# Block sums of the squared-ReLU activations made by GpSimd in the first MLP product and kept in DRAM, instead of made by VectorE in the second

## The chip, the cores and the metric

The kernel runs on one core of one Trainium2 chip. The metric is the device time of one execution in microseconds (us). Before the change it is 2887.82 us, the median of three runs (2886.27 to 2888.08).

The engines are PE (TensorE, matmul; PEld is its weight load), DVE (VectorE), ACT (ScalarE), POOL (GpSimd) and SP (SyncE, which here only issues DMAs). A DMA can be issued from SP, ACT or POOL; the profile calls those issued from POOL software DMAs.

## The reference

One inference step of a decoder trunk with two layers. Layer 0 is forgetting attention beside an RG-LRU, layer 1 is sparse attention with a lightning indexer. Each layer ends in the part that the change touches:

```python
def sq_relu_ffn(x, w1, w2):
    return jnp.square(jax.nn.relu(x @ w1)) @ w2

hp = hp + sq_relu_ffn(rms_norm(hp, norm_ffn[layer]), ffn_w1[layer], ffn_w2[layer])
hs = hs + sq_relu_ffn(rms_norm(hs, norm_ffn[layer]), ffn_w1[layer], ffn_w2[layer])
```

`hp` has 1024 prompt rows and `hs` 8 sample rows; the kernel puts them side by side, T = 1032 columns. D_MODEL is 1024, D_FF 4096, and all is fp32.

## The kernel before

The work runs with features on the partitions and the T = 1032 columns along the free dimension. Every fp32 product is made of three matmuls on fp32r halves: a value is split into hi (a rounded copy, made by ACT) and lo (value minus hi, a subtraction with two operands in SBUF, made by DVE or POOL), and the product is hi·hi + hi·lo + lo·hi (lines 1489 to 1491).

Both products of the MLP save one multiplication in eight with a Strassen-Winograd scheme: seven block products, numbered i = 0 to 6, in place of eight (`product`, line 1480). It needs sums and differences of blocks of the weights (`Left`, line 1357) and of the right operand. A column half is 2·HP = 516 columns: x1 the first 516, x2 the last.

**First product, "up"** (`up`, line 1522). Sixteen groups g, each of 256 output features, seven products each, 24 matmuls per product. Per group two raw weight tiles `fraw` of 512 KB are loaded by SP (line 1394), multiplied by the norm's gain on POOL (`up_scale`, line 1502, 128x1024), and made into operands `fl` and `fs` five products ahead (`up_make`). The results are evacuated from PSUM into two tiles of 128 features, `za` and `zb` (128x1032, lines 1547 to 1562, ACT and DVE), go through ReLU and the norm's scale on DVE, are squared on ACT (lines 1566 and 1570), and are stored to DRAM by SP as `d_z` (lines 1567 and 1571).

**Second product, "down"** (`down`, line 1659). Seven blocks b of 512 features (groups 2b and 2b+1), in each four outputs op, in each seven products of 12 matmuls: 28 products or 336 matmuls in a block. The last 512 features (groups 14 and 15) are multiplied plainly behind it. At the start of block b SP loads the four tiles `zr` of block b+1 (`z_load`, line 1575). During block b, after every fourth product, `z_make` (line 1580) makes one of the seven right operands of block b+1: it forms the block difference in place in `zr` on DVE where one is needed (i = 1, 2 and 3; eight 128x516 subtractions for each block, lines 1604, 1605, 1607 and 1611), copies hi on ACT (line 1608) and subtracts lo on POOL (line 1609; for block 0 by turns on DVE and POOL). The operands are `zop` (i = 0 to 2) and `zoph` (i = 3 to 6). The weights of block b+1 are prepared six products ahead (`down_make`, line 1615): their sums `s` and `fraw` on POOL (pattern "pppp"), hi on ACT, lo (`fd`, `fdu`, 128x256) on DVE. DVE also adds each product out of PSUM into the residual `xT` or `x1a`/`x1b` (line 1686, two 128x258 additions for each product).

**What sets the order.** The code emits one stream; a scheduler orders each engine's instructions by its own simulated times and gives out the buffers. An engine runs its instructions in that order and waits at the first that is not ready. Most tiles come out of one pool of 22 buffers (`U`, tag "u"): `fraw`, `fs`, `z`, `zr`, `zop`, `fdu` all share it, so that a load can wait for another tile's last reader. The helpers `act`, `tt`, `gt`, `stt` stand in lines 215 to 229 and are the lines by which the profile names ACT, DVE (L218, L229) and POOL (L221) work; `eng` (line 1353) picks POOL for "p" and DVE otherwise.

Of the kernel before, what the change touches and what calls it, by code (L numbers as in the profile page):

```python
# [75 lines left out]
def _r(ap):  # L76
    return ap.bitcast(F32)
# [13 lines left out]
UPLA, DNLA = 5, 6  # L91
ZSUB, ZADD = ("dp" * 7, "p" * 14), ("d" * 7, "d" * 7)
UPE, DNE = ("dddd", "ddddddd"), ("pppp", "ddddddd")
# [66 lines left out]
def build(tc, I, O, C):  # L160
    nc = tc.nc
    with ExitStack() as ctx:
# [1301 lines left out]

        d_z = [dr.tile([32, 128, T], F32, name="d_z%d" % l) for l in range(2)]

        class Ffn:
# [12 lines left out]
            def product(self, ps, left, right, start):  # L1480

                wh, wl = left
                nk = len(right)
                for p in range(2):
                    for k in range(nk):
                        hi, lo = lohi(right[k])
                        cols = slice(p * HP, p * HP + HP)
                        o = ps[p][:, :HP]
                        mm(o, lhsT=wh[:, k], rhs=hi[:, cols], start=(start and k == 0), stop=False, skip_group_check=not start)  # L1489
                        mm(o, lhsT=wh[:, k], rhs=lo[:, cols], start=False, stop=False, skip_group_check=not start)  # L1490
                        i = mm(o, lhsT=wl[:, k], rhs=hi[:, cols], start=False, stop=(k == nk - 1),  # L1491
                               skip_group_check=not start)
                dense[0] = i.ins.name
                return 6 * nk * HP / 2.4


# [25 lines left out]
            def up(self, before):  # L1522
# [3 lines left out]
                for g in range(16):  # L1526
# [3 lines left out]
                    for z, i in enumerate((0, 3, 1, 2, 4, 5, 6) if g == 0 else range(7)):  # L1530
# [33 lines left out]
                        if i == 5:  # L1564
                            stt(za, za, 0.0, rb, MAX, MUL)
                            act(za, za, AF.Square)
                            dma(out=d_z[self.l][2 * g], in_=za)
                        if g == 15:
                            before(z)
                    act(zb, zb, AF.Square)  # L1570
                    dma(out=d_z[self.l][2 * g + 1], in_=zb)
                    self.lefts.pop(g)


            def z_load(self, b):
                q = self.zq[b] = [U([128, T], F32, "zr") for _ in range(4)]
                for j in range(4):
                    dma(out=q[j], in_=d_z[self.l][4 * b + j])

            def z_make(self, b, i):  # L1580
                if i == 0:
                    self.zs[b] = {}
                s = self.zs[b]

                def alloc(i):
                    if i < 3:
                        s[i] = [U([128, T], F32R, "zop") for _ in range(2)]
                    else:
                        if i in (3, 4):
                            h, x = H(F32R, "zoph"), (3, 4)  # L1590
                        else:
                            h, x = H(F32R, "zoph"), (5, 6)
                        for y in range(2):
                            s[x[y]] = [h[:, 2 * y + j] for j in range(2)]

                x1, x2 = slice(0, 2 * HP), slice(2 * HP, 4 * HP)
                for k in {0: (0,), 1: (1,), 2: (2,), 3: (3,), 5: (5,)}.get(i, ()):
                    alloc(k)
                for j in range(2):
                    za, zb = self.zq[b][2 * j], self.zq[b][2 * j + 1]  # L1600
                    src = (za[:, x1], za[:, x1], za[:, x1], zb[:, x1], za[:, x2], zb[:, x2], zb[:, x1])[i]
                    hi, lo = lohi(s[i][j])
                    if i == 1:
                        eng(ZADD[b > 0], i)(za[:, x1], za[:, x2], za[:, x1], SUB)
                        eng(ZADD[b > 0], i)(za[:, x2], zb[:, x2], za[:, x2], SUB)
                    elif i == 2:
                        eng(ZADD[b > 0], i)(za[:, x1], zb[:, x2], za[:, x1], SUB)
                    act(hi, src)
                    eng(ZSUB[b > 0], 2 * i + j)(lo, src, _r(hi), SUB)
                    if i == 3:  # L1610
                        eng(ZADD[b > 0], i)(zb[:, x1], zb[:, x1], za[:, x1], SUB)
                if i == 6:
                    self.zq.pop(b)

# [27 lines left out]
            def before(self, z):  # L1642

                if z == 0:
                    self.zq, self.zs, self.dn_made, self.du = {}, {}, 0, {}
                    self.z_load(0)
                    self.r2.load(1)
# [11 lines left out]
            def down(self):  # L1659
                for i in range(4, 7):  # L1660
                    self.z_make(0, i)
                for b in range(7):
                    if b < 6:
                        self.z_load(b + 1)
                    for op in range(4):
# [4 lines left out]
                        for i in range(7):  # L1670
                            self.down_make(7 * m + i + DNLA)
                            if b < 6 and (7 * op + i) % 4 == 3:
                                self.z_make(b + 1, (7 * op + i) // 4)
                            if i == 1:
# [15 lines left out]
                    if b == 5:  # L1690
# [4 lines left out]
                        for k in range(4):  # L1695
                            dma(out=_r(zl[k]), in_=d_z[self.l][28 + k])
                    if b == 6:
# [916 lines left out]
```

## Time and profile before

| | |
|---|---|
| time, median of 3 runs | 2887.82 us (2886.27 to 2888.08) |
| profiled execution: time, span | 2877.05 us, 2875.2 us |
| busy share of the span | PE 90%, PEld 84%, DVE 76%, ACT 47%, POOL 41% |
| mean granted clock of TensorE | 0.948 of full speed |
| chain that ended last | PE 48%, DVE 23% of the span; its largest DVE entry is `DVE zr L218` with 4% |
| layer 0: up, down | up from about 636 to 958 us, down to about 1298 us |
| layer 1: up, down | up from about 2140 to 2471 us, down to about 2816 us |
| DMA | 318.91 MB, 111 GB/s over the span |

Times below are microseconds from the span's start. A row of a view by windows has the busy time of each engine with its number of instructions in brackets, then the granted clock of TensorE (1.00 is 2.4 GHz, 0.50 is 1.2 GHz), the busy share of the DMA engines, and GB/s. A row of a view by groups has the line, engine, operation, output and inputs, shapes and count, then busy us and mean ns of one, then the idle time of the engine in front of them and what ended it. A row of a timeline has start, duration, engine, line, operation, and in brackets the idle time before it.

### The profile page before, as it was taken

The numbers are of one execution on the slowest core, as the hardware profiler recorded it, in microseconds if no ns is written. First come the engines' busy times: TensorE is split into PE (matmuls) and PEld (weight loads), VectorE is DVE, ScalarE is ACT, GpSimd is POOL, SyncE is SP. The second block draws the span as 40 slices with busy tenths as digits, with TensorE's granted clock in tenths as the row PEclk, the third lists the DMA queues.
The fourth block names the chain that finished last, engine by engine and source line by source line (L and its number), as shares of the span: only waits on it lengthen the run. The fifth ranks groups of instructions, "written<-read, shape, count | busy, mean of one in ns | idle before, by whom it ended". The sixth has DMA issues, their size and how long they took to land.

```text
span 2875.2 us, 48325 instructions
## 1 busy us (share of the span) xinstructions
PE 2576.8 (90%) x17916; PEld 2406.7 (84%) x17916; DVE 2195.1 (76%) x4243; ACT 1341.9 (47%) x2824; POOL 1191.2 (41%) x916
## 2 busy tenths in 40 slices
PE   7988888989999888899888758999969999889998
PEld 6977878979999888899877744567969999788898
DVE  4467897787566999996468899998386565999995
ACT  4236656344343433333255567779244444433331
POOL 2375554242222676730544525033041121667740
PEclk9999899989999999999989868999989999999999
DMA  4854567203232422222353335210313232432221
GB/s 130 265 157 130 162 210 266 95 30 109 98 118 89 147 90 97 89 96 92 89 159 109 113 85 131 75 56 23 111 38 110 97 118 89 133 103 82 96 89 60
DMA packets 254400, 318.91 MB, mean 111 GB/s; under 512 B 23617, under 2 KB 198889, under 8 KB 253909
## 3 DMA queue, kind: packets, MB, share of 16 engines
q1 hardware_dynamic: 207492, 275.68, 29.7%
q10 hardware_dynamic: 39616, 19.93, 2.4%
q0 software_dynamic: 7056, 20.22, 2.4%
q8 instruction: 141, 2.31, 0.3%
q14 instruction: 95, 0.77, 0.1%
HBM read 230.00 MB, written 85.81 MB: 110 GB/s over the span
## 4 chain that ended last, share of the span: by engine, by line
PE 48%; DVE 23%; issue 4%; ACT 3%; DMA 1%; POOL 1%; SPq 0%; DVEq 0%; ACTq 0%; POOLq 0%
PE d L1489 10%; PE d L1491 10%; PE d L1490 10%; DVE zr L218 4%; PE d L341 3%; PE d L339 3%; PE d L340 3%; DVE xT L218 2%; DVE fdu L218 2%; PE s L530 2%; DVE fd L218 2%; PE o L2081 2%; PE t L251 1%; DVE x1a L218 1%; DVE tjk L1975 1%
## 5 line engine op out<-in xcount | busy, mean ns | idle before, releaser
L221 POOL TENSOR_TENSOR fraw<-fraw,small 128x1024 f32<-128x1024 f32 x64 | 142.0, 2227 | 424.4 <-DMA fraw<-in_ffn_w 193.9
L1489 PE MATMUL d<-xoph,fs 128*128 128x258 f32 x768 | 219.0, 285 | 5.9 <-ACT z L215 4.9
L218 DVE TENSOR_TENSOR xT<-xT,d 128x258 f32<-128x258 f32 (+1 forms) x472 | 186.7, 423 | 45.8 <-PE d L341 31.4
L1490 PE MATMUL d<-xoph,fs 128*128 128x258 f32 x768 | 218.8, 285 | 2.6 <-DVE xoph L218 2.6
L1491 PE MATMUL d<-xoph,fs 128*128 128x258 f32 x768 | 218.6, 285 | 2.4 <-DVE fs L218 2.4
L339 PE MATMUL d<-xh,whif 128*128 128x344 f32 (+1 forms) x616 | 202.8, 330 | 5.7 <-DVE small L226 2.4
L341 PE MATMUL d<-xh,wlof 128*128 128x344 f32 (+1 forms) x616 | 198.9, 327 | 6.6 <-DVE wlof L218 6.6
L340 PE MATMUL d<-xl,whif 128*128 128x344 f32 (+1 forms) x616 | 200.9, 326 | 0.0
L215 ACT ACTIVATE s<-s,small 128x128 f32<-128x128 f32 (+7 forms) x192 | 149.5, 781 | 69.5 <-DVE small L533 68.8
L339 PE MATMUL d<-xh,whi 128*128 128x344 f32 x504 | 170.9, 340 | 11.0 <-ACT whi L215 5.5
L341 PE MATMUL d<-xh,wlo 128*128 128x344 f32 x504 | 165.7, 332 | 11.8 <-DVE wlo L218 11.6
L340 PE MATMUL d<-xl,whi 128*128 128x344 f32 x504 | 167.8, 333 | 0.0
L221 POOL TENSOR_TENSOR zoph<-zr,zoph 128x516 fp32r<-128x516 f32 x104 | 156.9, 1522 | 25.5 <-ACT zoph L215 24.6
L1489 PE MATMUL d<-xop,fl 128*128 128x258 f32 x512 | 147.9, 289 | 14.6 <-ACT fl L215 14.6
L1489 PEld LDWEIGHTS d<-xoph,fs 128*128 128x128 f32 x768 | 146.2, 190 | 7.0 <-ACT z L215 5.7
L1491 PEld LDWEIGHTS d<-xoph,fs 128*128 128x128 f32 x768 | 146.7, 191 | 2.9 <-DVE fs L218 2.8
L251 PE MATMUL t<-small,s 128*128 128x128 f32 x864 | 139.8, 280 | 10.4 <-DVE tm L218 3.0
L1490 PEld LDWEIGHTS d<-xoph,fs 128*128 128x128 f32 x768 | 146.4, 191 | 3.2 <-DVE xoph L218 3.2
L1491 PE MATMUL d<-xop,fl 128*128 128x258 f32 x512 | 146.7, 288 | 2.5 <-DVE fl L218 2.5
L1490 PE MATMUL d<-xop,fl 128*128 128x258 f32 x512 | 147.1, 287 | 0.0
L1489 PE MATMUL d<-zoph,fdu 128*128 128x258 f32 x448 | 133.1, 298 | 13.6 <-DVE xT L218 8.4
L221 POOL TENSOR_TENSOR zop<-zr,zop 128x516 fp32r<-128x516 f32 x78 | 117.2, 1512 | 63.4 <-ACT zop L215 36.9
(482 smaller groups left out, 9850.2 us busy)
## 6 DMA issues: line engine op xcount, KB each, us to landing
fraw<-in_ffn_w SPq DMA_DIRECT2D x120, 512.0 KB
d_z<-z SPq DMA_DIRECT2D x64, 516.0 KB
zr<-d_z SPq DMA_DIRECT2D x56, 516.0 KB
kp<-in_cache_fox_kv SPq DMA_DIRECT2D x64, 256.0 KB
vp<-in_cache_fox_kv SPq DMA_DIRECT2D x64, 256.0 KB
q1b<-d_q ACTq DMA_DIRECT2D x32, 512.0 KB
wraw<-in_ab_w_in SPq DMA_DIRECT2D x21, 512.0 KB
wrawf<-in_c_w_in SPq DMA_DIRECT2D x17, 512.0 KB
```

The costliest lines, as they stand in the source:

```text
L215: return nc.scalar.activation(out=out, in_=in_, func=func, **kw)
L218: return nc.vector.tensor_tensor(out=out, in0=a, in1=b, op=op)
L221: return nc.gpsimd.tensor_tensor(out=out, in0=a, in1=b, op=op)
L251: return nc.tensor.transpose(out, in_, ident[:n, :n])
L339: mm(ps, lhsT=wh, rhs=ah, start=(j == 0), stop=False)
L340: mm(ps, lhsT=wh, rhs=al, start=False, stop=False)
L341: i = mm(ps, lhsT=wl, rhs=ah, start=False, stop=(j == last))
L530: mm(p[:, :m], lhsT=lh[x], rhs=ks[:, k0:k0 + m], start=(x == 0), stop=(x == 1 and not dg))
L1489: mm(o, lhsT=wh[:, k], rhs=hi[:, cols], start=(start and k == 0), stop=False, skip_group_check=not start)
L1490: mm(o, lhsT=wh[:, k], rhs=lo[:, cols], start=False, stop=False, skip_group_check=not start)
L1491: i = mm(o, lhsT=wl[:, k], rhs=hi[:, cols], start=False, stop=(k == nk - 1), skip_group_check=not start)
L2081: mm(po[:64], lhsT=VF[g // 2][:, kb, 64 * (g % 2):64 * (g % 2) + 64], rhs=ph, start=(kb == 0), stop=(kb == i))
```

## The change

The plain blocks and the sums are now made once, in the first product, and stored side by side as `d_zp`: for each block b seven slots of 128 x 2 x 516, one for each right operand (the 2 are the groups 2b and 2b+1). In group g < 14, SP stores the first half of `za` (slot 0) and both halves of `zb` (slots 1 and 2); then POOL makes four subtractions 128x516 in place in `za` and `zb` (`z_sums`), and POOL itself issues two DMAs that store the four results (slots 3 to 6). Groups 14 and 15 are stored plainly as before.

In the second product `z_load` fetches one slot (128x1032, 516 KB) for one operand, a few operands ahead (ZLA = 3), and `z_make` has only the hi copy on ACT and the lo subtraction left, each one instruction of 128x1032 in place of two of 128x516. The subtraction is POOL's for b > 0; for block 0 DVE and POOL take turns. The eight DVE subtractions on `zr` per block are gone. A block is read from DRAM as seven tiles of 516 KB instead of four.

```diff
-ZSUB, ZADD = ("dp" * 7, "p" * 14), ("d" * 7, "d" * 7)
+ZSUB, ZLA = ("dpdpdpd", "p" * 7), 3
...
-        d_z = [dr.tile([32, 128, T], F32, name="d_z%d" % l) for l in range(2)]
+        d_z = [dr.tile([4, 128, T], F32, name="d_z%d" % l) for l in range(2)]
+        d_zp = [dr.tile([7, 7, 128, 2, 2 * HP], F32, name="d_zp%d" % l) for l in range(2)]
+        ZSLOT = (0, 3, 6, 1, 4, 2, 5)
...
-                        hi, lo = lohi(right[k])
+                        hi, lo = right[k] if type(right[k]) is tuple else lohi(right[k])
...
+            def zp(self, g, s, n):
+                v = d_zp[self.l][g // 2, s:s + n, :, g % 2]
+                return v[0] if n == 1 else v.rearrange("i p c -> p i c")
+            def z_sums(self, g, za, zb):
+                if g >= 14:
+                    dma(out=d_z[self.l][2 * g - 27], in_=zb)
+                    return
+                x1, x2 = slice(0, 2 * HP), slice(2 * HP, 4 * HP)
+                two = lambda z: z.rearrange("p (i c) -> p i c", i=2)
+                dma(out=self.zp(g, 1, 2), in_=two(zb))
+                gt(za[:, x1], za[:, x2], za[:, x1], SUB)
+                gt(za[:, x2], zb[:, x2], za[:, x2], SUB)
+                nc.gpsimd.dma_start(out=self.zp(g, 3, 2), in_=two(za))
+                gt(zb[:, x2], zb[:, x2], za[:, x1], SUB)
+                gt(zb[:, x1], zb[:, x1], zb[:, x2], SUB)
+                nc.gpsimd.dma_start(out=self.zp(g, 5, 2), in_=two(zb))
...
-                            dma(out=d_z[self.l][2 * g], in_=za)
+                            if g < 14:
+                                dma(out=self.zp(g, 0, 1), in_=za[:, :2 * HP])
+                            else:
+                                dma(out=d_z[self.l][2 * g - 28], in_=za)
...
-                    dma(out=d_z[self.l][2 * g + 1], in_=zb)
+                    self.z_sums(g, za, zb)
...
-            def z_load(self, b):
-                q = self.zq[b] = [U([128, T], F32, "zr") for _ in range(4)]
-                for j in range(4):
-                    dma(out=q[j], in_=d_z[self.l][4 * b + j])
+            def z_load(self, n):
+                while self.zn < min(n, 49):
+                    b, i = divmod(self.zn, 7)
+                    t = self.zq[b, i] = U([128, 2, 2 * HP], F32, "zr")
+                    dma(out=t, in_=d_zp[self.l][b, ZSLOT[i]])
+                    self.zn += 1
             def z_make(self, b, i):
...
+                s = self.zs.setdefault(b, {})
+                if i < 3:
+                    hi, lo = (U([128, 2, 2 * HP], F32R, "zop") for _ in range(2))
+                else:
+                    if i in (3, 5):
+                        self.zh2 = H(F32R, "zoph").rearrange("p k (j c) -> p k j c", j=2)
+                    y = (i - 3) % 2
+                    hi, lo = self.zh2[:, 2 * y], self.zh2[:, 2 * y + 1]
+                s[i] = [(hi[:, j], lo[:, j]) for j in range(2)]
+                self.z_load(7 * b + i + 1)
+                src = self.zq.pop((b, i))
+                act(hi, src)
+                eng(ZSUB[b > 0], i)(lo, src, _r(hi), SUB)
...
-                    self.zq, self.zs, self.dn_made, self.du = {}, {}, 0, {}
-                    self.z_load(0)
+                    self.zq, self.zs, self.dn_made, self.du, self.zn = {}, {}, 0, {}, 0
+                    self.z_load(4)
...
+                self.z_load(7 + ZLA)
                 for b in range(7):
-                    if b < 6:
-                        self.z_load(b + 1)
...
-                                self.z_make(b + 1, (7 * op + i) // 4)
+                                n = (7 * op + i) // 4
+                                self.z_make(b + 1, n)
+                                self.z_load(7 * (b + 1) + n + 1 + ZLA)
...
```

What stands where before and now, at two places. The names carry buffer numbers; the semaphores in brackets are those an instruction waits for (DMAHW: DMAs issued from SP or ACT; DMASW: DMAs issued from POOL; DVE, Activation, PE, Pool: these engines).

First place: POOL in the middle of the first product of layer 0, before (two groups' scalings of raw weights and half of two more):

```order
L221 TENSOR_TENSOR fraw_7845<-fraw_7845,small_75 128x1024 [waits DMAHW0_49,DMAHW2_49,DVE_49,PE_49]
L221 TENSOR_TENSOR fraw_7847<-fraw_7847,small_75 128x1024 [waits DMAHW1_49,DVE_49,Pool_49]
L221 TENSOR_TENSOR fraw_8076<-fraw_8076,small_75 128x1024 [waits DMAHW4_49,DMAHW6_49,DVE_49,PE_49]
L221 TENSOR_TENSOR fraw_8078<-fraw_8078,small_75 128x1024 [waits DMAHW5_49,DVE_49,Pool_49]
L221 TENSOR_TENSOR fraw_8307<-fraw_8307,small_75 128x1024 [waits DMAHW0_49,DMAHW2_49,DVE_49,PE_49]
```

and now, one group's scalings, the sums of the group two earlier and their two stores:

```order
L221 TENSOR_TENSOR fraw_7883<-fraw_7883,small_75 128x1024 [waits DMAHW0_49,DMASW5_49]
L221 TENSOR_TENSOR fraw_7885<-fraw_7885,small_75 128x1024 [waits DMAHW1_49,DMASW6_49]
L221 TENSOR_TENSOR z_7650<-z_7650 128x516 [waits DMAHW2_49,Activation_49]
L221 TENSOR_TENSOR z_7650<-z_7651,z_7650 128x516 [waits Activation_49,Pool_49]
L221 TENSOR_TENSOR z_7651<-z_7651,z_7650 128x516 [waits DMAHW3_49,Pool_49]
L1513 DMA d_zp0_122<-z_7650 128x2x516
L221 TENSOR_TENSOR z_7651<-z_7651 128x516 [waits DVE_49,Pool_49]
L1516 DMA d_zp0_122<-z_7651 128x2x516 [waits Pool_49]
```

Between two pairs of scalings POOL now has four subtractions and two DMA issues. On SP at the same place, before:

```order
L1394 DMA fraw_7845<-in_ffn_w1 128x4x256 [waits DMAHW2_49,DMAHW0_49,PE_49]
L1394 DMA fraw_7847<-in_ffn_w1 128x4x256 [waits DMAHW1_49,DVE_49,Pool_49]
L1567 DMA d_z0_120<-z_7618 128x1032 [waits Activation_49]
L1571 DMA d_z0_120<-z_7619 128x1032 [waits Activation_49]
L1394 DMA fraw_8076<-in_ffn_w1 128x4x256 [waits DMAHW6_49,DMAHW4_49,PE_49]
```

and now:

```order
L1394 DMA fraw_7883<-in_ffn_w1 128x4x256 [waits DMAHW0_49,DMASW5_49,Pool_49]
L1394 DMA fraw_7885<-in_ffn_w1 128x4x256 [waits DMAHW1_49,DMAHW7_49,DMASW6_49,Pool_49]
L1590 DMA d_zp0_122<-z_7650 128x516 [waits DMAHW2_49,Activation_49]
L1510 DMA d_zp0_122<-z_7651 128x2x516 [waits DMAHW3_49,Activation_49]
L1394 DMA fraw_8120<-in_ffn_w1 128x4x256 [waits DMAHW4_49,DMASW7_49,Pool_49]
```

The loads of the next raw weights, which waited for PE, DVE and POOL, now wait for DMASW, that is for POOL's stores of `z` to have landed: they take the buffers of that `za` and `zb`. They stand in front of the next group's stores on SP.

Second place: the second product of layer 0 while the operands of the block b = 3 are made. On DVE before:

```order
L218 TENSOR_TENSOR xT0_4698<-xT0_4698,d_11359 128x258 [waits PE_49]
L218 TENSOR_TENSOR zr_11349<-zr_11349 128x516 [waits DMAHW6_49,Pool_49]
L218 TENSOR_TENSOR xT0_4698<-xT0_4698,d_11360 128x258 [waits PE_49]
L218 TENSOR_TENSOR fd_11523<-fraw_11210,fd_11523 128x256 [waits Activation_49]
L218 TENSOR_TENSOR zr_11351<-zr_11351 128x516 [waits DMAHW0_49,Pool_49]
L218 TENSOR_TENSOR xT1_4699<-xT1_4699,d_11212 128x258 [waits PE_49]
L218 TENSOR_TENSOR zr_11349<-zr_11350,zr_11349 128x516 [waits DMAHW7_49,DVE_49]
L218 TENSOR_TENSOR xT1_4699<-xT1_4699,d_11213 128x258 [waits PE_49]
```

and now, at the same weights of the operand before (the tile named fraw_11210 is fraw_11254 now):

```order
L218 TENSOR_TENSOR fdu_11453<-fraw_11254,fdu_11453 128x256 [waits Activation_49]
L218 TENSOR_TENSOR xT0_4700<-xT0_4700,d_11395 128x258 [waits PE_49]
L218 TENSOR_TENSOR fd_11494<-fraw_11254,fd_11494 128x256 [waits Activation_49]
L218 TENSOR_TENSOR xT0_4700<-xT0_4700,d_11396 128x258 [waits PE_49]
L218 TENSOR_TENSOR fd_11555<-fraw_11254,fd_11555 128x256 [waits Activation_49]
L218 TENSOR_TENSOR xT1_4701<-xT1_4701,d_11256 128x258 [waits PE_49]
L218 TENSOR_TENSOR xT1_4701<-xT1_4701,d_11257 128x258 [waits PE_49]
```

The subtractions on `zr` are gone from between the additions to `xT` and the lo parts `fd` and `fdu`. On POOL at the same place, before:

```order
L221 TENSOR_TENSOR fraw_11210<-s1_11413,fraw_11210 128x2x128 [waits DVE_49,Pool_49]
L221 TENSOR_TENSOR zop_11420<-zr_11349,zop_11420 128x516 [waits DMAHW6_49,Activation_49]
L221 TENSOR_TENSOR zop_11421<-zr_11351,zop_11421 128x516 [waits DMAHW0_49,Activation_49]
L221 TENSOR_TENSOR zoph_11664<-zr_11350,zoph_11664 128x516 [waits DMAHW7_49,Activation_49]
L221 TENSOR_TENSOR zoph_11664<-zr_11352,zoph_11664 128x516 [waits DMAHW1_49,Activation_49]
L221 TENSOR_TENSOR fraw_11210<-fraw_11210 128x2x128 [waits DVE_49,Pool_49]
L221 TENSOR_TENSOR zop_11499<-zr_11349,zop_11499 128x516 [waits PE_49,Activation_49]
L221 TENSOR_TENSOR zoph_11824<-zr_11350,zoph_11824 128x516 [waits PE_49,Activation_49]
L221 TENSOR_TENSOR zoph_11824<-zr_11352,zoph_11824 128x516 [waits Activation_49]
```

and now:

```order
L221 TENSOR_TENSOR fraw_11254<-s1_11449,fraw_11254 128x2x128 [waits DVE_49,Pool_49]
L221 TENSOR_TENSOR zop_11457<-zr_11221,zop_11456 128x1032 [waits DMAHW6_49,Activation_49]
L221 TENSOR_TENSOR zop_11536<-zr_11299,zop_11535 128x1032 [waits DMAHW0_49,Activation_49]
L221 TENSOR_TENSOR fraw_11254<-fraw_11254 128x2x128 [waits DVE_49,Pool_49]
L221 TENSOR_TENSOR zoph_11694<-zr_11460,zoph_11694 128x1032 [waits DMAHW3_49,PE_49,Activation_49]
L221 TENSOR_TENSOR zoph_11694<-zr_11539,zoph_11694 128x1032 [waits DMAHW5_49,Activation_49]
L221 TENSOR_TENSOR s1_11591<-fraw_11393 128x256 [waits DMAHW2_49,PE_49]
```

Fourteen subtractions 128x516 have become seven of 128x1032, in nearly the same stretch between the weights' sums (`s1` and `fraw`).

## Rows read from the trace of the kernel before

**Rows 1.** Busy time of each engine in four windows of layer 0.
```profile
700.00:740.00 40.00, 40.00 (x335) 40.00 (x335) 25.70 (x43) 17.11 (x32) 9.07 (x4) 1.00 0.32 114
958.80:1006.00 47.20, 38.65 (x270) 35.77 (x269) 47.20 (x83) 21.51 (x48) 39.48 (x33) 0.93 0.36 119
1195.50:1243.00 47.50, 43.74 (x338) 43.14 (x338) 45.36 (x94) 18.09 (x42) 34.59 (x31) 0.93 0.21 68
1243.00:1283.00 40.00, 40.00 (x337) 40.00 (x336) 35.30 (x85) 15.40 (x31) 9.79 (x13) 1.00 0.27 94
```

**Rows 2.** The same view, windows of 4 us in a block of layer 1.
```profile
2680.00:2684.00 4.00, 0.60 (x6) 0.43 (x4) 4.00 (x5) 1.16 (x2) 4.00 (x4) 0.90 0.00 0
2684.00:2688.00 4.00, 4.00 (x19) 4.00 (x20) 4.00 (x8) 1.05 (x3) 4.00 (x4) 0.50 0.00 0
...
2712.00:2716.00 4.00, 4.00 (x36) 4.00 (x35) 3.02 (x9) 1.25 (x3) 0.74 (x1) 1.00 1.00 340
```

**Rows 3.** Chain of waits in 950 to 1270: shares, and two pieces.
```profile
by line: DVE zr L218 19.1%; DVE xT L218 16.7%; PE d L1489 12.3%; PE d L1490 11.8%; PE d L1491 11.8%; DVE fdu L218 8.9%; issue 8.6%; DVE fd L218 7.6%; DVE z L229 1.0%; ACT fdu L215 0.7%; DVE zoph L218 0.5%; DVE z L218 0.5%; ACT fd L215 0.3%;
...
1116.68 1.79 DVE zr L218
...
1164.09 1.79 DVE zr L218
```

**Rows 4.** Groups by shape on DVE, 960 to 1240 (second product, layer 0).
```profile
L218 DVE TENSOR_TENSOR xT<-xT,d 128x258 f32<-128x258 f32 x313 | 118.6, 413 | 7.4 <-PE d L1491 7.3
L218 DVE TENSOR_TENSOR zr<-zr 128x516 f32<-128x516 f32 x50 | 64.1, 1282 | 0.0
L218 DVE TENSOR_TENSOR fdu<-fraw,fdu 128x256 fp32r<-128x256 f32 x71 | 47.9, 678 | 0.0
L218 DVE TENSOR_TENSOR fd<-fraw,fd 128x256 fp32r<-128x256 f32 x70 | 46.6, 668 | 0.1
```

**Rows 5.** Groups by shape on POOL in the same window.
```profile
L221 POOL TENSOR_TENSOR zoph<-zr,zoph 128x516 fp32r<-128x516 f32 x49 | 74.3, 1531 | 12.2 <-ACT zoph L215 11.9
...
L221 POOL TENSOR_TENSOR fraw<-fraw 128x256 f32<-128x256 f32 x47 | 40.6, 866 | 17.4 <-DVE fd L218 16.1
```

**Rows 6.** Timeline of DVE late in a block of layer 1.
```profile
2707.13 0.41 DVE L218 TENSOR_TENSOR fdu<-fraw,fdu 128x256 fp32r<-128x256 f32 x1
2707.47 0.41 DVE L218 TENSOR_TENSOR fd<-fraw,fd 128x256 fp32r<-128x256 f32 x1
```

**Rows 7.** Timelines of POOL and of DVE in the first product, layer 1.
```profile
2269.69 1.90 POOL L221 TENSOR_TENSOR fraw<-fraw,small 128x1024 f32<-128x1024 f32 x1 [1.84 <-DMA fraw<-in_ffn_w]
...
2269.80 2.33 DVE L218 TENSOR_TENSOR fl<-fraw,fl 128x512 fp32r<-128x512 f32 x1 [1.29 <-ACT fl L215]
```

**Rows 8.** Instructions of the tiles zr and r1l: lo parts on POOL, ns min/median/max.
```profile
L221 POOL TENSOR_TENSOR zoph<-zr,zoph x104: 1277/1478/2287, 949.1 to 2746.2; 128x516 fp32r<-128x516 f32 x104
...
L221 POOL TENSOR_TENSOR r1l<-raw,r1h x12: 2387/2429/2449, 1397.4 to 1627.6; 128x1032 fp32r<-128x1032 f32 x12
```

**Rows 9.** Timelines of SP, POOL, ACT and DVE in the first product, layer 0.
```profile
750.09 0.94 SPq L1394 DMA_DIRECT2D fraw<-in_ffn_w  x2
757.36 0.34 SPq L1567 DMA_DIRECT2D d_z<-z  x1
...
770.25 0.94 SPq L1394 DMA_DIRECT2D fraw<-in_ffn_w  x2
...
754.34 5.27 POOL L221 TENSOR_TENSOR fraw<-fraw,small 128x1024 f32<-128x1024 f32 x2 [24.65 <-DMA fraw<-in_ffn_w]
...
760.14 0.64 ACT L215 ACTIVATE fs<-fraw 128x512 fp32r<-128x512 f32 x1 [0.26 <-DMA d_z<-z]
...
767.34 0.69 DVE L218 TENSOR_TENSOR s<-fraw 128x512 f32<-128x512 f32 x1 [0.97 <-PE d L1490]
```

**Rows 10.** Line 865: POOL's own DMAs of 512 KB in the attention of layer 0.
```profile
L865 POOL DMA_DIRECT2D qst<-d_q x16: 713/735/781, 90.2 to 480.6; - x16
...
DMA to landing us min/median/max: 4.3/7.7/11.1
```

More of the change, by code (lines that the diff above doesn't have):

```diff
@@ L1570, in up @@
                     act(zb, zb, AF.Square)
-                    dma(out=d_z[self.l][2 * g + 1], in_=zb)
+                    self.z_sums(g, za, zb)
                     self.lefts.pop(g)
-            def z_load(self, b):
-                q = self.zq[b] = [U([128, T], F32, "zr") for _ in range(4)]
-                for j in range(4):
-                    dma(out=q[j], in_=d_z[self.l][4 * b + j])
-            def z_make(self, b, i):
[L1581 to L1613, printed above, removed]
@@ L1695, in down @@
                         for k in range(4):
-                            dma(out=_r(zl[k]), in_=d_z[self.l][28 + k])
+                            dma(out=_r(zl[k]), in_=d_z[self.l][k])
                     if b == 6:
```

## The prediction

> **What bounds the kernel now.** I read the windows by stage first, then the chain of waits, then the groups and timelines of the engines that end a wait. In the first product PE is busy without a gap: 335 matmuls in 40 us, 0.1194 us each, with DVE at 25.7 and POOL at 9.1 of 40 us [rows 1]. Nothing there is won by making DVE lighter, and whatever is added there must stay hidden. In the second product a block is 336 matmuls, 40.1 us at that rate. The last block, which prepares no successor, reaches it (337 in 40 us). The blocks before it take 47.4 us: the window 1195.5 to 1243 holds 338 matmuls in 47.5 us with DVE busy for 45.4 and POOL for 34.6 [rows 1], and in the chain the same `zr` subtraction comes back 47.4 us later (1116.68, 1164.09) [rows 3]. Preparing the next block thus costs 7.3 us.
>
> How it costs that is seen in windows of 4 us: PE gets 6 matmuls while DVE and POOL are both busy throughout; then, PE having stood, the granted clock is 0.50 (the level of 1.2 GHz) for 4 us with 19 matmuls [rows 2]. The chain names DVE: `zr` has 19.1% of 320 us, 61 us, more than any other line [rows 3]. So DVE is what ends last, and `zr` is what the change takes from it.
>
> **Second product, what goes.** Per block DVE does 56 additions out of PSUM, 28 lo parts `fd`/`fdu` and 8 `zr` subtractions. The `zr` group has 1.282 us each, 10.3 us per block. The additions keep 0.413 us, but `fd` and `fdu` take 0.68 on average [rows 4], while two of them undisturbed take 0.41 and start 0.34 apart [rows 6]. So POOL holds each of the 28 up by some 0.26, 7.3 us per block.
>
> **Second product, what changes.** POOL's fourteen lo parts of 128x516 (1.53 us) become seven of 128x1032; its 16 weight sums per block (0.87) stay [rows 5]. The long form is in the trace elsewhere, 2.43 us where DVE is quiet; the short form has 1.28 at its fastest [rows 8], so beside a busy DVE I add the same 0.23 to the long one: 2.66. POOL goes from 14 x 1.53 + 16 x 0.87 = 35.3 us per block to 7 x 2.66 + 13.9 = 32.5. POOL is not the bound.
>
> The point that speaks against the change is what a longer POOL instruction does to DVE. In one place DVE's `fl`, 0.69 us alone [rows 9], took 2.33 because a POOL instruction of 1.90 us had started 0.11 before it [rows 7]: it waited 1.64 us, nearly all of it. The Trainium skill, SBUF — State Buffer, section "SBUF: two separate sides", says that a DVE instruction with two SBUF inputs and a GpSimd one lock each other out for a whole instruction and do not share the port; this place agrees. If the port were shared instead, the wait would go with POOL's busy time and fall to 6.7 us per block, and PE alone would bound the block.
>
> With whole instructions waited for, the wait per `fd` grows with the number of POOL instructions times their length squared, over the block's time. Before: 14 x 1.53² = 32.8 and 16 x 0.87² = 12.1, so 73% of the 7.3 us come from `z` parts. After: 7 x 2.66² = 49.5, and the block is nearer 41.5 than 47.4 us. The `z` share grows by 1.72, the rest by 1.14: 7.3 x (0.73 x 1.72 + 0.27 x 1.14) = 11.4 us. DVE's block is then (56 + 28) x 0.335 + 11.4 = 39.5 us. Before, DVE was busy 45.4 of 47.5 us, so 2.1 us went idle while the block was bound by it; I keep them: 41.6. Bounds: if no `fd` waits longer than now, DVE has 28.1 + 7.3 + 2.1 = 37.5 and PE's 40.1 stands; if each of the seven long ones holds DVE for the 86% seen at `fl`, the wait is 7 x 2.29 + 2.2 = 18.2, and the block is 48.4, 1 us worse than now. I take 41.6, 5.8 us less per block, nearer to the PE end because DVE's own `zr` work is gone for certain.
>
> Five blocks in each of two layers (b = 1 to 5): 10 x 5.8 = 58 us. I take layer 1 as layer 0; rows 2, of layer 1, show the same stall. Block 0 is worse now: 270 matmuls (32.2 us) in 47.2 us with DVE busy for all of it [rows 1], 15 us lost; 5.8 of them go likewise, 12 us for two layers. The sums of block 0 in front of it go from DVE too; I count nothing there (0 to 8 us).
>
> Reading 7 x 516 + 4 x 512 KB per block is 137 GB/s, where a window shows 340 [rows 2]; loads run three operands ahead, each operand being due every four products (5.7 us). SP issues three loads more per block and ACT has fewer instructions: nothing for either. Hidden under the matmuls; if that cover went, the operand that is late would show as an ACT wait for `zr`.
>
> **First product, what is added.** Per group POOL gets four subtractions of about 1.3 to 1.5 us and two DMA issues of 0.74 [rows 8, 10], 7.1 us in 20.1, on top of 4.5 [rows 1]. DVE's two-input work can wait behind them, but the operands are made five products (14 us) ahead and DVE has 14 of 40 us free, so nothing is charged for that. Behind the subtractions on POOL stands the next scaling of `fraw`, and the load of that `fraw` on SP waits until POOL's stores have landed.
>
> The timing of that loop: a pair of loads was issued at 750.09, POOL scaled from 754.34 to 759.61, and the first use of the result was at 767.34 [rows 9]. So there are 7.7 us of slack. The sums come right behind the scaling: three subtractions, an issue, a fourth, an issue, so `zb` is issued at 759.6 + 4 x 1.4 + 0.74 = 766.0 and its buffer is free at 766.0 + X, X being landing. The load that takes it went out at 770.7. A full round is X + 6.4 (sums) + 4.3 (load to scaling) + 2.6 (one scaling): X + 13.3, against a period of 20.1; so X up to 6.8 is free. X is not in this stage's trace. Nearest rows: POOL's own DMAs of the same size have 4.3, 7.7 and 11.1 (least, median, most) [rows 10]; SP's store of 516 KB at 757.36 had landed by 760.14, 2.8 us [rows 9]. At 7.7 a round is 0.9 us too long: twelve rounds, 10.8 us less the slack of 7.7, 3 us per layer. I take that, 6 us in all; bounds 0 (X at 4.3) and, at 11.1, 12 x 4.3 - 7.7 = 44 per layer, 88.
>
> **The sum.** -58 - 12 + 6 = -64 us against the profiled execution's 2877.05 (span 2875.2, 1.9 us around it). That execution is 10.8 us under the median of the runs shown, 2887.82; the difference is carried over: 2824 us.
>
> **The rivals.**
> *PE alone bounds the second product.* DVE's relief is 10.3 us per block and 7.3 would do. Every block falls to 40.1: 10 x 7.3 + 2 x 12 (block 0 keeps 3 of its 15) and no loss in the first product, 97 us: 2791. For it: DVE does nothing on POOL's account in over half of a block [rows 6]. Against it: the work for the next block comes bunched, which is where PE stood [rows 2].
> *The long POOL instructions eat it.* A wait of 16 us gives DVE 28.1 + 16 + 2.1 = 46.2: 1.2 us per block, 12 us, 4 more in block 0, 6 lost: 2878. For it: `fl` [rows 7].
> *The stores through POOL set the pace of the first product.* Slower: PE, without a gap now, begins to wait for `fraw`, scaled too late because its buffer is still being stored. It decides from X = 9.8: 2 x (12 x (X - 6.8) - 7.7) then equals the 70 us won in the second product. At 11.1 it is 88 - 70 = 18 us slower, 2906. For it: half of POOL's DMAs took over 7.7 us [rows 10]. Against: when these stores go out, no weight load is in flight (they are issued 750 and 770, the stores about 763 and 766). The Trainium skill, same page and section, calls this a trap: descriptors of GpSimd's DMAs are written through that shared port, so that a store of 0.62 us stood 3.1 us beside a DVE copy. No row shows this by itself; by that 2.5 us more on 4.3, X would be 6.8, just at the edge.
>
> **How the numbers follow.** The forecast, 2805 to 2845, has 0.46. PE alone: 0.2. Long instructions: 0.18, spread over 2850 to 2895 with a third of it beyond no change. The loop: 0.14. 0.02 is for what I have not seen. 0.2% (6 us) is about what can be told from no change. Faster: 0.46 + 0.2 + 0.12 = 0.78; within 0.2%: 0.06; slower: 0.16. The range 2788 to 2893 leaves out the loop's cases and little below.
>
> **What would show it.** The second product's blocks should be 41 to 42 us long, `zr` absent from DVE, `fd` and `fdu` at 0.75 to 0.85 us mean, the clock at 1.00 in nearly every window. The additions out of PSUM should still be what PE waits for, if it waits. In the first product PE should stay at 335 in 40 us; POOL there should be at 23 of 40, and `fraw` should wait for its DMA with no PE gap behind. I am wrong if PE has gaps in the first product that end in POOL's scaling (the loop), if blocks stay at 45 us or more with `fd` above 0.9 (long instructions), or if an operand waits for its load of `zr`.

## The result, and the profile after

The median is 2848.53 us (4 runs, 2839.99 to 2850.07) against 2887.95: a ratio of 0.9866, interval 0.9854 to 0.9878, 39 us less where 64 were forecast. It lies 3.5 us outside the likeliest band of the prediction (2805 to 2845) and just short of the one of the rival with the long POOL instructions (2850 to 2895). By stage, from the starts of the matmuls in the two traces (the first product from its first matmul, 624.9 and 2124.9 us before and 628.9 and 2121.4 after; then end of one product to end of the next):

| us | before | after | change | forecast |
|---|---|---|---|---|
| first product, layers 0 and 1 | 333.8, 346.2 | 334.6, 345.9 | +0.5 | +6 |
| second product, layer 0 | 339.5 | 326.7 | -12.8 | -35 |
| second product, layer 1 | 344.6 | 318.2 | -26.4 | -35 |

That is -38.7, near the 39.4 between the medians. The two profiled executions differ by 27.7 only: ahead of, between and behind the two MLPs the later one took 11 us more. The profiled execution of the kernel before, 2877.05, stands among runs on a chip where the median was 2877.49; beside the changed kernel it was 2887.95. Between the MLPs, 826.7 became 831.3 us; further kernels with the order of the changed one there took 824 to 836. So the 11 us may be the chip or spread; no run tells them apart.

The view by windows, columns as in [rows 1]: a stretch of the first product, block 0 of layer 0, a steady block, the last block.

```profile
700.00:740.00 40.00, 40.00 (x335) 40.00 (x335) 29.40 (x43) 16.28 (x30) 23.84 (x17) 1.00 0.49 164
963.40:1020.80 57.40, 45.59 (x340) 43.55 (x338) 54.63 (x91) 24.85 (x47) 37.10 (x28) 0.94 0.54 184
1111.10:1155.90 44.80, 41.49 (x338) 40.63 (x338) 42.31 (x85) 17.44 (x36) 30.07 (x24) 1.00 0.34 116
1246.20:1286.20 40.00, 40.00 (x333) 40.00 (x332) 35.47 (x80) 14.22 (x24) 6.80 (x9) 1.00 0.24 71
```

In this window the first product is as full as before, with POOL at 23.8 of 40. A steady block is 44.8 us, between the 47.4 of [rows 3] and the 41.6 forecast. Its parts, windows of 4 us:

```profile
1114.00:1118.00 4.00, 2.93 (x24) 2.75 (x24) 4.00 (x8) 1.19 (x3) 2.90 (x3) 1.00 0.32 117
1118.00:1122.00 4.00, 3.21 (x27) 3.01 (x26) 4.00 (x7) 0.49 (x1) 4.00 (x2) 1.00 0.01 2
...
1130.00:1134.00 4.00, 2.57 (x21) 2.26 (x20) 4.00 (x7) 1.12 (x2) 4.00 (x3) 1.00 0.00 0
...
1142.00:1146.00 4.00, 4.00 (x35) 4.00 (x34) 3.49 (x10) 1.56 (x4) 2.27 (x3) 1.00 0.03 9
...
1150.00:1154.00 4.00, 4.00 (x35) 4.00 (x35) 2.73 (x8) 0.71 (x3) 1.32 (x2) 1.00 0.46 130
```

The loss lies where POOL makes its `z` parts: in three such windows PE gets 21 to 27 of 35 matmuls, and DVE is busy throughout. Later in the block PE is full and DVE has time left. PE's gaps are shorter than in [rows 2], and the clock stays at 1.00. What PE's matmuls waited for in five steady blocks of layer 1 (us in total, times, longest) was DVE's additions, and neither POOL nor a load:

```profile
PE d L1491 <- DVE x1a L218: 16.3, 17, 1.5
```

The chain over 950 to 1270, as [rows 3]: `zr` is gone, `fdu` has its place, and one piece comes back every 44.8 us.

```profile
by line: PE d L1491 19.4%; PE d L1493 18.5%; PE d L1492 18.5%; DVE fdu L218 15.1%; DVE xT L218 10.4%; issue 8.7%; DVE fd L218 5.1%; POOL zoph L221 1.6%; DVE zoph L218 0.9%; DVE z L229 0.6%; POOL zop L221 0.5%; DVE z L218 0.3%; POOL s L221 0
...
1066.31 3.22 DVE fdu L218 x2
1111.08 3.21 DVE fdu L218 x2
...
1155.86 3.20 DVE fdu L218 x2
```

Groups by shape on DVE, then on POOL, 960 to 1240, as [rows 4, 5]:

```profile
L218 DVE TENSOR_TENSOR xT<-xT,d 128x258 f32<-128x258 f32 x325 | 122.9, 414 | 13.0 <-PE d L1493 12.1
L218 DVE TENSOR_TENSOR fdu<-fraw,fdu 128x256 fp32r<-128x256 f32 x75 | 76.8, 1036 | 0.0
L218 DVE TENSOR_TENSOR fd<-fraw,fd 128x256 fp32r<-128x256 f32 x74 | 53.1, 720 | 0.2
```

```profile
L221 POOL TENSOR_TENSOR zoph<-zr,zoph 128x1032 fp32r<-128x1032 f32 x25 | 64.0, 2570 | 1.0 <-ACT zoph L215 1.0
```

`fdu` went from 0.68 to 1.04 us. One of them on DVE beside POOL's `zoph`, both ending within 0.3 us (a line of DVE's timeline and one of POOL's):

```profile
1129.49 2.65 DVE L218 TENSOR_TENSOR fdu<-fraw,fdu 128x256 fp32r<-128x256 f32 x1
...
1129.24 2.62 POOL L221 TENSOR_TENSOR zoph<-zr,zoph 128x1032 fp32r<-128x1032 f32 x1
```

The first product on SP and POOL:

```profile
753.59 3.57 SPq L1394 DMA_DIRECT2D fraw<-in_ffn_w  x2
...
752.70 0.73 POOL L1516 DMA_DIRECT2D d_zp<-z  x1 [0.30 <-POOL z L221]
758.35 1.92 POOL L221 TENSOR_TENSOR fraw<-fraw,small 128x1024 f32<-128x1024 f32 x1 [4.93 <-DMA fraw<-in_ffn_w]
```

The second of SP's two loads takes the buffer that POOL's store of `zb` leaves. An issue takes 0.37 us on SP, so it went out at 756.8, 4.1 us after the store's issue began at 752.70. That is X: 4.1, and 4.9 and 4.0 in the next two groups, where I took 7.7. By the semaphores in the trace all 28 such stores landed 3.2 to 6.2 us after their issue began, half of them within 3.4.

### The profile page after: what moved, and what is told of

It reads as the page before. It is cut to its first block, busy times and chain, and to the rows that moved or that the text cites. A ratio compares the mean times of both kernels' runs of the same rounds, so it can differ in the third digit from the quotient of the medians.

```text
span 2847.5 us, 48497 instructions
## 1 busy us (share of the span) xinstructions
PE 2560.3 (90%) x17916; PEld 2391.2 (84%) x17916; DVE 2245.4 (79%) x4125; ACT 1330.8 (47%) x2726; POOL 1339.5 (47%) x992
## 4 chain that ended last, share of the span: by engine, by line
PE 49%; DVE 20%; issue 5%; ACT 3%; DMA 2%; POOL 2%; SPq 0%; DVEq 0%; POOLq 0%; another core or an unknown queue 0%; ACTq 0%
PE d L1491 11%; PE d L1492 10%; PE d L1493 10%; DVE fdu L218 4%; PE d L341 3%; PE d L339 3%; PE d L340 3%; PE s L530 2%; PE t L251 2%; PE o L2089 1%; DVE xT L218 1%; DVE tjk L1983 1%; DVE x1a L218 1%; PE o L2093 1%; DVE fd L218 1%
## 5 line engine op out<-in xcount | busy, mean ns | idle before, releaser
L221 POOL TENSOR_TENSOR z<-z 128x516 f32<-128x516 f32 x112 | 170.5, 1522 | 32.2 <-DMA d_zp<-z 21.9
L218 DVE TENSOR_TENSOR fdu<-fraw,fdu 128x256 fp32r<-128x256 f32 x168 | 161.3, 971 | 0.0
L1491 PEld LDWEIGHTS d<-xoph,fs 128*128 128x128 f32 x768 | 145.9, 190 | 10.3 <-ACT z L215 9.0
L1491 PE MATMUL d<-zoph,fdu 128*128 128x258 f32 x448 | 129.4, 291 | 23.8 <-DVE xT L218 12.1
```

Of the source, the lines that this page charges most:

```text
L218: return nc.vector.tensor_tensor(out=out, in0=a, in1=b, op=op)
L221: return nc.gpsimd.tensor_tensor(out=out, in0=a, in1=b, op=op)
```

## The experiments

A: a DVE instruction with two SBUF inputs waits for the end of the POOL instruction that runs. B: the wait goes by POOL's total busy time. C: something else holds the blocks. The blocks below are steady ones of layer 1; the wait is 28 times the mean of `fd` and `fdu` less 0.41 us, and POOL's busy time is of the same blocks. The chips differ a little: beside the first four kernels before took 2877.49 us, beside the next four 2884.92, beside the last two 2886.42. So the ratios compare. "No lo parts" and "before, no `zr` sums" leave work out of the computation: they price that work and are no kernels to use.

| kernel | block | wait | POOL busy | ratio to before, interval |
|---|---|---|---|---|
| before | 47.4 | 7.0 | 34.0 | 1 |
| changed | 44.7 | 12.8 | 29.7 | 0.9866 (0.9854 to 0.9878) |
| lo parts in 2 pieces | 41.1 | 10.0 | 32.0 | 0.9708 (0.9686 to 0.973) |
| in 4 pieces | 40.4 | 7.3 | 34.4 | 0.9721 (0.9705 to 0.9737) |
| lo parts on DVE | 40.9 | 2.7 | 13.6 | 0.9773 (0.9748 to 0.9797) |
| no lo parts | 40.3 | 1.3 | 12.0 | 0.9638 (0.9615 to 0.966) |
| before, no `zr` sums | 41.3 | 9.9 | 31.5 | 0.9769 (0.9747 to 0.979) |
| before, 4 pieces | 44.5 | 6.5 | 37.9 | 0.9874 (0.9855 to 0.9893) |

**Two pieces.**
```diff
-                eng(ZSUB[b > 0], i)(lo, src, _r(hi), SUB)
+                if b:
+                    for j in range(2):
+                        gt(lo[:, j], src[:, j], _r(hi[:, j]), SUB)
+                else:
+                    eng(ZSUB[0], i)(lo, src, _r(hi), SUB)
```


> The lo part of z in the second product is made by POOL in two pieces of 128x516 in place of one of 128x1032 (blocks 1 to 6); all else is as in the changed kernel (2848.5 us, steady block 44.8 us). A (a DVE instruction with two SBUF inputs waits for the end of the POOL instruction that runs, so shorter ones cost less): fd and fdu fall from 0.87 us mean to 0.65 to 0.75, the wait from 12.8 to some 8 us per block, the block to 40.5 to 42.5, and the time to 2806 to 2826. B (the wait goes with POOL's total busy time): POOL is busy some 3 us longer per block, so blocks of 44.8 to 45.5 us, 2848 to 2856. C (the blocks are held by something other than DVE's waits, by the loads or the order): blocks 44.8, 2848.

2794.48 us; by its ratio 2804 where before takes 2887.95, just below A's range, with the block inside it. Block 0, which the expectation left alone, fell too (57.3 to 49.1 and 50.9 to 47.0 us): POOL makes the operands of block 1 there. The wait is 10.0 and `fd` and `fdu` are 0.77 on average, where A had some 8 and 0.65 to 0.75. POOL is busier than in the changed kernel and the wait is shorter: B and C fall. A block, and the groups on DVE in four blocks, 2525.3 to 2689.6:

```profile
2566.40:2607.40 41.00, 40.53 (x338) 40.33 (x337) 39.39 (x85) 17.42 (x36) 32.16 (x31) 1.00 0.44 143
```

```profile
L218 DVE TENSOR_TENSOR fdu<-fraw,fdu 128x256 fp32r<-128x256 f32 x49 | 39.1, 802 | 0.0
L218 DVE TENSOR_TENSOR fd<-fraw,fd 128x256 fp32r<-128x256 f32 x49 | 36.0, 736 | 0.1
```

**Lo parts on DVE.**
```diff
-ZSUB, ZLA = ("dpdpdpd", "p" * 7), 3
+ZSUB, ZLA = ("dpdpdpd", "d" * 7), 3
```


> The seven lo parts of z per block go from POOL to DVE (blocks 1 to 6), where one takes 1.22 us, so DVE gets 8.1 us of work per block and POOL keeps its 16 weight sums of 0.78. A: the wait falls from 12.8 to 2.5 to 4 us per block, a little more than DVE gets; blocks of 41 to 43.5, 2811 to 2836. B: the wait falls by POOL's busy time, from 12.8 to 5.4, less than DVE gets: blocks of 45.5, 2855. C: 44.8 to 46, 2848 to 2860.

2811.01 us, blocks of 40.9, just under A's 41 to 43.5, and the wait inside A's range: DVE does more work and is still the sooner done. Its total is behind that of two pieces for another reason: the scheduler's order between the MLPs came out otherwise, and that stretch took 846 us in place of 826.

**No lo parts.**
```diff
-                eng(ZSUB[b > 0], i)(lo, src, _r(hi), SUB)
+                if b:
+                    act(lo, src)
+                else:
+                    eng(ZSUB[0], i)(lo, src, _r(hi), SUB)
```

> The lo part of z is left out for blocks 1 to 6: ACT copies the operand into the lo tile (1.05 us each, seven per block), so neither DVE nor POOL has any work for z. It is the floor of the second product with z free of cost. A and B: DVE has 28.1 us of work and 3 to 5 us of waits per block, so PE alone bounds: blocks of 40.1 to 40.6, 2801 to 2806. C: blocks stay at 43 us or more, 2830 to 2848.

2772.28 us, well below the range; a block is 40.3, nearly the 40.1 of PE alone. Blocks 1 to 5 fell by 45.8 us in the two layers, as expected; what the expectation left out is block 0, from 57.3 to 43.4 us in layer 0 and from 50.9 to 44.7 in layer 1. A steady block with DVE at 33.0, then block 0 of layer 0, whose DVE was 54.6 us busy in the changed kernel (windows as above):

```profile
2545.50:2585.90 40.40, 40.40 (x339) 40.40 (x338) 32.99 (x85) 23.86 (x43) 12.06 (x16) 1.00 0.45 146
...
961.90:1005.30 43.40, 41.23 (x338) 40.44 (x337) 40.87 (x96) 32.20 (x55) 17.93 (x20) 1.00 0.73 243
```

**Relief of DVE alone.** In the kernel before, for b > 0:
```diff
-                    if i == 1:
+                    if b:
+                        pass
+                    elif i == 1:
...
-                    if i == 3:
+                    if i == 3 and not b:
```


> The kernel before, with the eight zr subtractions of each block left out for blocks 1 to 6 (the differences are not formed; loads, hi and lo parts as before). It is the relief of DVE alone, with the short POOL instructions of 128x516. A: the wait stays at 7 us per block, DVE has 28.1 + 7 + some 3.5, so blocks of 40.1 to 42 us in place of 47.4, 2815 to 2834. B: the same POOL time as before, so the same. C, or if DVE's relief is worth no more than the changed kernel got: blocks of 44.8, 2855 to 2862.

2809.40 us, blocks of 41.3: the relief is worth 6.1 us per block with short POOL instructions. The changed kernel got 2.7. The 3.4 between them are the price of the long ones, and two pieces get them back. A's wait was wrong here: 9.9, not 7; why it grew by so much in the shorter block stays open. A block:

```profile
2576.30:2617.70 41.40, 40.95 (x339) 40.52 (x338) 39.65 (x85) 17.84 (x44) 31.96 (x31) 1.00 0.31 103
```

**Four pieces.** Against two pieces:
```diff
-                        gt(lo[:, j], src[:, j], _r(hi[:, j]), SUB)
+                        for h in (slice(0, HP), slice(HP, 2 * HP)):
+                            gt(lo[:, j, h], src[:, j, h], _r(hi[:, j, h]), SUB)
```

> The lo part of z in four pieces of 128x258 (blocks 1 to 6), where the run before it had two of 128x516 and blocks of 41.0 us; the floor with no work for z was 40.3. A (a DVE instruction with two SBUF inputs waits for the end of the POOL instruction that runs): the wait falls again, from 8.9 us per block to 5 to 7, and the block to 40.4 to 40.8, some 4 us in all: 2786 to 2793. B (the wait goes by POOL's busy time, which grows with the pieces): blocks of 41 to 42 us, 2794 to 2805.

Blocks of 40.4, A's lower edge, where B had 41 to 42; the wait, 7.3, is just over A's 5 to 7. The total, 2806.32 us, missed A's range and is no better than that of two pieces: the stretch between the MLPs took 852 us, with the same shift of order as above. So it is the blocks that decide for A here, not the total.

**Block 0 too.**
```diff
-ZSUB, ZLA = ("dpdpdpd", "p" * 7), 3
+ZSUB, ZLA = ("dp" * 7, "p" * 14), 3
...
-                eng(ZSUB[b > 0], i)(lo, src, _r(hi), SUB)
+                for j in range(2):
+                    eng(ZSUB[b > 0], 2 * i + j)(lo[:, j], src[:, j], _r(hi[:, j]), SUB)
```

> The lo part of z in pieces of 128x516 in block 0 too, where DVE and POOL take turns piece by piece; blocks 1 to 6 as in the run with two pieces (2794.5 us; block 0 is 49.1 and 47.0 us there). A: POOL's long instructions are gone from block 0 as well, where they fell on DVE work; block 0 falls by 1 to 3 us in each layer: 2789 to 2793. If block 0 is held by DVE's sheer amount of work: no change, 2793 to 2797.

2800.69 us, 0.9718 (0.9687 to 0.9749): nothing won. Block 0 was 50.4 and 48.8 us, no shorter than with two pieces (49.1 and 47.0), so its own lo parts do not hold it. But neither does the amount of DVE's work, the other case of the expectation: with the same work on DVE it was 57.3 and 50.9 us in the changed kernel, 46.7 and 45.9 in four pieces and 43.4 and 44.7 without lo parts. It falls as the POOL instructions for block 1's operands get shorter or go.

**Stores issued by SP.** Against two pieces (the store of `zb` likewise):
```diff
-                nc.gpsimd.dma_start(out=self.zp(g, 3, 2), in_=two(za))
+                dma(out=self.zp(g, 3, 2), in_=two(za))
```

> As the run with two pieces, but the two stores of sums per group in the first product are issued by SP and not by POOL. Theory: stores through POOL land in about 4 us (SP's next load of raw weights goes out that long after them), so they pace nothing: the first products stay at 334 and 345 us, 2791 to 2798 in all. Rival (they cost something after all): the short gaps of the first product go and each layer wins 1 to 2 us. Rival (SP's own order): the stores wait on SP for POOL's sums, the loads behind them are late, and PE gets gaps: 2 to 20 us slower.

2797.18 us, 0.9695 (0.9677 to 0.9713): no difference in the total. The first products were 332.4 and 341.7 us against 334.2 and 345.2. Layer 1's gain shows again in the run "Together" below (341.7), layer 0's does not (335.0), so POOL's issue had a small price in layer 1, as the first rival had it.

**Sums made by DVE.** Against two pieces (all four likewise):
```diff
-                gt(za[:, x1], za[:, x2], za[:, x1], SUB)
+                tt(za[:, x1], za[:, x2], za[:, x1], SUB)
```

> As the run with two pieces, but the four subtractions per group in the first product are made by DVE and not by POOL, which still issues the stores. DVE is busy for some 31 of 40 us there; it gets four of 0.7 us per 20 us and loses the waits behind POOL's sums. Theory (POOL's sums are hidden, and so would DVE's be): the first products stay at 334 and 345 us, 2791 to 2798. Rival (POOL's sums cost the gaps seen there by delaying DVE): 1 to 2 us less per layer. Rival (DVE's sums stand in front of the evacuation that PE waits for): 3 to 20 us slower.

2801.98 us, 0.9708 (0.9692 to 0.9725), the ratio of two pieces; the first products were 332.6 and 345.4. The sums cost nothing that shows on either engine.

**Together.** SP's stores, and four pieces except in block 1 of layer 0, which keeps the order between the MLPs:
```diff
+                    w = HP if self.l or b > 1 else 2 * HP
                     for j in range(2):
-                        gt(lo[:, j], src[:, j], _r(hi[:, j]), SUB)
+                        for h in range(0, 2 * HP, w):
+                            gt(lo[:, j, h:h + w], src[:, j, h:h + w], _r(hi[:, j, h:h + w]), SUB)
```

> The two things that the runs point to, together: lo parts of z in four pieces of 128x258 (blocks 1 to 6; in layer 0 block 1 keeps two of 128x516), and the stores of sums issued by SP. With two pieces and SP's stores it was 0.9695 of the kernel before. A (a DVE instruction with two SBUF inputs waits for the end of the POOL instruction that runs): blocks of 40.4 in both layers in place of 41.05, 6 us, and some 3 us less in blocks 0 and 1: a ratio of 0.966 to 0.968. B (POOL's busy time decides): 0.970 or more.

2795.67 us, 0.9677 (0.966 to 0.9695): the best ratio, though not apart from two pieces with SP's stores. Steady blocks were 40.3, but block 1 of layer 1 took 51.6. Its DVE, then its POOL:

```profile
2492.32 8.11 DVE L218 TENSOR_TENSOR fdu<-s,fdu 128x256 fp32r<-128x256 f32 x1 [2.36 <-ACT fdu L215]
```

```profile
2491.80 1.46 POOL L221 TENSOR_TENSOR zoph<-zr,zoph 128x258 fp32r<-128x258 f32 x2
...
2493.92 2.79 POOL L221 TENSOR_TENSOR zop<-zr,zop 128x258 fp32r<-128x258 f32 x4
2496.69 0.71 POOL L221 TENSOR_TENSOR fraw<-s,fraw 128x256 f32<-128x256 f32 x1
2497.37 2.79 POOL L221 TENSOR_TENSOR zoph<-zr,zoph 128x258 fp32r<-128x258 f32 x4
```

**Before, four pieces.** In the kernel before:
```diff
-                    eng(ZSUB[b > 0], 2 * i + j)(lo, src, _r(hi), SUB)
+                    if b > 1 or b and self.l:
+                        for h in (slice(0, HP), slice(HP, 2 * HP)):
+                            gt(lo[:, h], src[:, h], _r(hi[:, h]), SUB)
+                    else:
+                        eng(ZSUB[b > 0], 2 * i + j)(lo, src, _r(hi), SUB)
```

> The kernel before, with the lo parts of z in pieces of 128x258 in place of 128x516 (blocks 1 to 6, in layer 0 blocks 2 to 6); the eight zr subtractions stay on DVE. It tells whether short POOL instructions alone would have done. A: the wait falls from 7 to some 5 us per block, DVE still has 28.1 + 10.3 us of its own, so blocks of 44.5 to 46 us in place of 47.4, and 0.990 to 0.995 of the kernel before. Rival (the wait is all that held the blocks, zr none of it): blocks of 41 us, 0.978.

2851.30 us, blocks of 44.5, A's lower edge, and a ratio below its 0.990 to 0.995; the wait is 6.5, where A had some 5. Short instructions alone, or the moved sums as the change has them, give about 3 us per block; together 7. Part of it here is `zr`, from 1.32 to 1.06 us: it has two SBUF inputs as well.

## Why the prediction was right in sign and too large

- **Steady blocks, 5.8 us forecast.** From the starts of blocks 1 and 6, five blocks fell from 240.1 to 225.4 us in layer 0 and from 239.5 to 223.6 in layer 1: -30.6, not -58. This is the step that failed: DVE's time per block was put at 41.6 us and is 44.7. Of the 3.1 us, 1.4 are the wait, which grew as foreseen in kind, but to 12.8 and not 11.4: in the two layers 167 of 392 `fd` and `fdu` took over 0.55 us (163 before), and such a one waited 0.99 us on average (0.57 before). Another 1.3 are DVE's own work. The prediction took 0.335 us for each of 84 instructions, the spacing of two undisturbed ones; in the steady block from 2563.0 us the 56 additions hold DVE for 19.7 us, 0.352 each, and the 28 lo parts with their waits for 22.5. The last 0.4 is idle time, 2.5 us and not 2.1. In the kernel before, the same sum had come out (28.1 + 10.3 + 7.0 + 2.1 = 47.5 for 47.4) because its errors cancelled; in the block from 1112.2 us the additions held DVE for 19.4 us and not 18.8, `zr` for 10.0 and not 10.3, the lo parts for 15.9 and not 16.4.
- **The rival "long POOL instructions eat it"** had the right mechanism. It ate over half of the relief (3.4 of 6.1 us), not all. "PE alone" was refuted for this kernel, and is nearly true in two or four pieces.
- **Block 0, -12.** The forecast was 6 us less in each layer, and neither had it. In layer 0 block 0 was 1.7 us longer. In layer 1, from the end of the first product, it went from 58.9 to 51.0. Together -6. The clock does not explain layer 0 (0.94 in the window above, 0.93 in [rows 1]). The long POOL instructions do in part: the 33 `fd` and `fdu` of that block took 34.8 us together; when the lo parts of block 1 came in two pieces, 32 took 28.3, and block 0 was 49.1 and not 57.3. The last 2.5 lie in the last block of layer 1, which the prediction did not count.
- **First product, +6.** It was +0.5, and X is 3.2 to 6.2 us, under the 6.8 that are free. So the loop does not bind, and the rival of the stores falls. (Its own formula decides from X = 10.4; at the 9.8 of the prediction it gives 57 us, not 70.) But the +0.5 depends on where the border is put: the kernel before began layer 1's second product with 12 matmuls of the first left. Counted to the first matmul of the second product, the first took 333.9 and 341.9 us before and 334.7 and 346.0 after, +4.9, and block 0 changed by -10.5. With the stores issued by SP, layer 1 is back at 341.8 in both kernels that have it; with POOL's it was 345.0 to 346.5 in seven. So POOL's stores have a price of some 4 us there, but not by the loop that was forecast; by what way stays open. The Trainium skill, SBUF — State Buffer, section "SBUF: two separate sides", has a trap for DMAs issued by GpSimd beside a DVE copy, and the estimate worked out from it was an X of 6.8. The 28 landings do not show it; but DVE ran no copies in this stage, only instructions with two inputs each (655 to 935 us), so this is no test of that trap.
- **Profile signs.** `zr` off DVE, clock, PE and POOL in the first product: as said. `fd` and `fdu`: 0.89 us in 960 to 1240, over the 0.75 to 0.85. The two signs of being wrong for the long instructions, blocks of 45 us and `fd` above 0.9, were missed by little: 44.8 and 0.89. The sign of an operand that waits for its load of `zr` did appear, but small: ACT waited for the load of `zr` 8 times in the 98 operands of the run, 6.3 us in all and at most 2.1, and PE's matmuls did not wait for it.

## What to carry to other kernels

When work is moved to an engine that holds up another one, look at the length of its instructions, not only at its busy share: the same subtraction in pieces of 1.4 us in place of 2.6 was worth 3.6 us per block, with more POOL time in all. And a sum that takes each instruction at the spacing of an undisturbed place can come out too low: with the measured wait it gives 28.1 + 12.8 + 2.1 = 43.0 us here, where the block is 44.7. Take the mean inside the block, and look for the stretch in which the engine is late.

## What the runs showed of the hardware

The Trainium skill, SBUF — State Buffer, section "SBUF: two separate sides", says that the one that starts first has the shared port for its whole instruction. The pair at 1129 us above agrees: the `fdu`, 0.25 us behind the `zoph`, ended 0.3 us after it. But a short DVE instruction need not get in at the next boundary of POOL's instructions. In the last rows above an `fdu` that takes 0.41 us alone lasted 8.11: POOL ran its instructions without a gap from 2491.80 to 2500.16, and DVE went on at 2500.36. It was the only one of that kernel's 392 that waited for so many: of the 239 that took over 0.55 us, 215 waited for the end of one POOL instruction, 22 for two and one for three. So A holds for most, not for all. PE stood, the clock fell to 0.65 in 2502 to 2510, and the block lost 11 us. The profiled run alone shows it; whether other executions of that kernel have it stays open.
